# SBUF tiles placed by size, and gate columns with both parts of the activations as one moving operand

## The chip, the core and the metric

One core of a Trainium2 chip runs the whole program. The metric is the device time of one execution in microseconds; of the kernel before there are three runs, 811.55, 812.54 and 812.93 us, median 812.54. A profiled execution took 812.01 us. TensorE (PE) multiplies, with weight loads of its own (PEld), VectorE (DVE) and ScalarE (ACT) do the elementwise work, GpSimd (POOL) helps out, SyncE (SP) issues most transfers.

## What is computed

Two residual layers over 256 tokens of width 2048, in float32, then a norm. Each layer normalises x, projects it, runs an attention over 32 heads of 64, multiplies the result by a SiLU gate that is a further projection z of the same input, and projects back:

```python
def mixer_a(h, w_in, sinks, w_out, cos, sin):
    proj = h @ w_in
    q, k, v, z = jnp.split(proj, [A_WIDTH, A_WIDTH + A_KV_WIDTH, A_WIDTH + 2 * A_KV_WIDTH], axis=-1)
    ...
    o = banded_attention(q, k, v, A_WINDOW, A_QBLOCK, sinks.reshape(A_KV_HEADS, A_GROUP))
    ...
    return (o * jax.nn.silu(z)) @ w_out

def reference(x, ...):
    for i in range(DEPTH):
        h = rmsnorm(x, norm_w[i])
        out = mixer_a(h, ...) if i == 0 else mixer_b(h, ...)
        x = x + out.astype(x.dtype)
    return rmsnorm(x, final_norm_w)
```

Layer B (`mixer_b`) has an attention with three branches (compressed, selected, windowed) and three more pairs of key and value columns, and the same gate z of 2048 columns. Both layers have 2048 columns of q and 2048 of z.

## The kernel before

Products are made in a two-part form of float32: a value v is split into hi, rounded to the matmul's own format (fp32r), and lo = v - hi, and a product is hi x hi + lo x hi + hi x lo, three matmuls that accumulate in one PSUM bank. The activations are kept transposed, in 16 k tiles of 128 rows: `hT` is the layer's normalised input (hT_hi and hT_lo, two tiles of 16 KB a partition), `aT` the gated attention output (aT_hi, aT_lo).

Weights stream. A step (`add_steps`, L559) covers 2 k tiles and 512 columns: one transfer of 512 KB into `raw` (four buffers, issued four steps ahead on SP's queue), an ACT copy into `w_hi` and a DVE subtraction into `w_lo` (three buffers each, two steps ahead, `split`, L541), then two halves of matmuls. A block is 8 steps that fill two banks `acc0` and `acc1`; there are three `acc` banks in all. After the last step a function `post` drains each bank.

Two kinds of blocks exist. A "tok" block (q, key, value and output columns) puts 128 tokens of hT or aT into the array as the stationary operand and streams 512 columns of w. A "feat" block (the gate columns z) is to come out transposed: 128 columns of w are stationary and the 256 tokens of hT_hi or hT_lo are streamed, so a half does for each of its two groups of 128 columns:

```python
for f in range(2):
    fc = (2 * b + f) * P
    PE.matmul(ps[:, f * S:(f + 1) * S], w_[:, fc:fc + P], hT[ai][:, kt, :],
              start=first and f == 0, stop=last, skip_group_check=True)
```

`post_z` (L668) drains such a bank with one DVE product by rbc (the norm's scale, by token), an ACT tanh and a DVE combination.

The order of the program is: layer A's key and value block; for g = 0 to 3 a q block and a z block; four output blocks with aT; layer B's three key and value blocks, with the small projections of its compression between them; again four times q and z; four output blocks. The attention of group g runs in the background, piece by piece behind the half steps (`background`, L469), mostly during the z block of g and the q block that follows. Everything is first recorded and then ordered by a planner (`Plan.order`), which plays the engines with prices and starts on each engine what is ready, in the order of recording; the big matmuls have the lowest rank (`plan.early = LAST`), so the attention goes first where both are ready. On the chip each engine then runs its list in order and waits on semaphores.

SBUF tiles are placed one behind another in the order in which they are first used. So the small ones among them shift the large ones: in the built program hT_hi, hT_lo, w_hi and w_lo start at 256 modulo 512 bytes, raw and x at 192, the key tile kT, qT and sm at 32, aT_hi and aT_lo at 352.

Of the kernel before, what the change touches and what calls it, by code (L numbers as in the profile page):

```python
# [12 lines left out]
F32 = mybir.dt.float32  # L13
# [177 lines left out]
class Plan:  # L191
# [140 lines left out]
def trunk(ctx: ExitStack, tc: tile.TileContext, x, positions, norm_w, final_norm_w,  # L332
# [182 lines left out]
    def hT_pair(i, hT, j):  # L515

        tb = t_bank("xT")
        for k in range(2):
            for t in range(NT):
                PE.transpose(tb[:, 2 * k + t, :], xt[t][:, (2 * j + k) * P:(2 * j + k + 1) * P], ident)  # L520
        src = [tb[:, 2 * k:2 * k + 2, :].rearrange("p a b -> p (a b)") for k in range(2)]
        g = [gT[:, i * KT + 2 * j + k:i * KT + 2 * j + k + 1] for k in range(2)]
        hi = [hT[0][:, 2 * j + k, :] for k in range(2)]
        for k in range(2):
            copy(hi[k], src[k], scale=g[k])
        for k in range(2):
            DVE.scalar_tensor_tensor(hT[1][:, 2 * j + k, :], src[k], g[k], hi[k].bitcast(F32),
                                     op0=OP.mult, op1=OP.subtract)
# [30 lines left out]
    def add_steps(w, width, col0, kind, act, post, before=None):  # L559

        blk = {}

        def mk(i):
            st = Step()
            st.cols = 1024
            st.dma = w_dma(w, i * 2 * P, 2, col0, NB, width)

            def half(b):  # L570
                if before:
                    before(i)
                hT = act()
                if i == 0:
                    blk[b] = acc_bank(f"acc{b}")
                ps = blk[b]
                for kk in range(2):
                    kt = 2 * i + kk
                    wh, wl = (w_[:, kk * NB:(kk + 1) * NB] for w_ in (st.hi, st.lo))
                    for pi, (ai, w_) in enumerate(((0, wh), (1, wh), (0, wl))):  # L580
                        first = kt == 0 and pi == 0
                        last = kt == KT - 1 and pi == 2
                        if kind == "tok":
                            plan.early = LAST
                            PE.matmul(ps, hT[ai][:, kt, b * P:(b + 1) * P], w_, start=first, stop=last)
                            plan.early = 0
                        else:
                            plan.early = LAST
                            for f in range(2):
                                fc = (2 * b + f) * P  # L590
                                PE.matmul(ps[:, f * S:(f + 1) * S], w_[:, fc:fc + P], hT[ai][:, kt, :],
                                          start=first and f == 0, stop=last, skip_group_check=True)
                            plan.early = 0
                if i == KT // 2 - 1:
                    post(b, ps)
            st.halves = [lambda: half(0), lambda: half(1)]
            return st
        for i in range(KT // 2):
            steps.append(mk(i))

# [67 lines left out]
    def post_z(layer, g):  # L668
        def post(b, ps):
            if b == 0:  # L670
                us[layer, g] = sb.tile([P, 4, S], F32, tag="u", name="u", bufs=2)
            u = us[layer, g][:, 2 * b:2 * b + 2, :]
            DVE.tensor_tensor(u, ps.rearrange("p (a b) -> p a b", a=2),
                              rbc[:, None, :].to_broadcast([P, 2, S]), op=OP.mult)
# [3 lines left out]
            if b == 1:  # L678
                flags.add(("z", layer, g))
        return post  # L680

# [173 lines left out]
    add_steps(a_w_in[0], A_IN, 2048, "tok", lambda: hT0,  # L855
              post_kv(0, lambda: kTA, (P, 0), lambda: vA), before=first_block)
    for g in range(NG):
        add_steps(a_w_in[0], A_IN, g * NB, "tok", lambda: hT0, post_q(0, g))
        add_steps(a_w_in[0], A_IN, 2560 + g * NB, "feat", lambda: hT0, post_z(0, g))
# [33 lines left out]
    for j in range(4):  # L893
        add_steps(a_w_out[0], D, j * NB, "tok", lambda: aTA, post_out_a(j),
# [178 lines left out]
    def add_gates():  # L1073
        box = {}

        def mk(i):
# [4 lines left out]
            def half(b):  # L1081
# [3 lines left out]
                for kk in range(4 * b, 4 * b + 4):  # L1085
                    kt = 8 * i + kk
                    wh, wl = (w_[:, kk * 96:(kk + 1) * 96] for w_ in (st.hi, st.lo))
                    for pi, (ai, w_) in enumerate(((0, wh), (1, wh), (0, wl))):
                        PE.matmul(ps[0:96, 0:S], w_, hT[ai][:, kt, :], start=kt == 0 and pi == 0,
# [14 lines left out]
    def b_add(col, kind, post, before=None):  # L1104
        add_steps(b_w_in[0], B_IN, col, kind, hT_b, post, before=before)
# [8 lines left out]
    for g in range(NG):  # L1114
        b_add(g * NB, "tok", post_q(1, g))
        b_add(3680 + g * NB, "feat", post_z(1, g))
# [126 lines left out]
    for j in range(4):  # L1243
        add_steps(b_w_out[0], D, j * NB, "tok", lambda: aTB[0], post_out_b(j),
                  before=out_before(1) if j == 0 else None)
# [91 lines left out]
```

## Time and profile before

| | us |
|---|---|
| runs, median of three | 812.54 |
| profiled execution, whole | 812.01 |
| profiled execution, span from first to last instruction | 810.3 |
| PE busy in the span | 791.3 |
| DVE busy | 546.1 |
| ACT busy | 469.6 |
| POOL busy | 132.1 |
| DMA, mean over the span | 159 GB/s |

Line 217 is the helper that emits every recorded instruction, so groups are told apart by the names of their tiles, out<-in; of a matmul the moving operand is named first and the stationary one second. Matmuls overlap, and a busy time of one, 398 ns, is longer than the distance to the next. That distance is read from starts in a timeline, or from a piece of the chain of waits: its length by its count.

### The profile page before, as it was taken

Reading aid. Unit: us, or ns where it says so; the run is one execution under the profiler, and the core shown is the slowest. Engines: PE = TensorE matmul, PEld = TensorE weight load, DVE = VectorE, ACT = ScalarE, POOL = GpSimd, SP = SyncE. Lnnn points to the kernel's source line nnn. Section 1 sums busy time; section 2 is a strip of 40 time slices with the busy share of each in tenths; the row PEclk is TensorE's granted clock in tenths of the full one; section 3 lists DMA queues with packets and bytes.
Section 4 is the critical chain, followed back from the end, with each engine's and each line's share of the span. In section 5 each row is a group of like instructions: output and inputs, shape, how many; then the busy total and the mean of one; then the engine's idle time right before and its main releaser. Section 6 shows DMA issues by size and latency. Waiting matters only on the chain.

```text
span 810.3 us, 12740 instructions
## 1 busy us (share of the span) xinstructions
PE 791.3 (98%) x4604; PEld 659.2 (81%) x4604; DVE 546.1 (67%) x1116; ACT 469.6 (58%) x931; POOL 132.1 (16%) x169
## 2 busy tenths in 40 slices
PE   7999999999999999999999999999999999999995
PEld 4889879799798788888878898788779769877884
DVE  5646957858668555555756478858948868875562
ACT  6658547456466344454756486567658748654442
POOL 2102211213023000020011022112221022211110
PEclk8999999999999999999999999999999999999998
DMA  8665454554553455565677654444444344454652
GB/s 268 196 177 170 130 170 143 156 157 130 158 180 131 155 182 182 179 190 171 178 228 210 173 163 119 131 131 131 108 143 140 106 130 131 156 156 134 192 168 104
DMA packets 69615, 128.83 MB, mean 159 GB/s; under 512 B 6178, under 2 KB 10497, under 8 KB 69424
## 3 DMA queue, kind: packets, MB, share of 16 engines
q1 hardware_dynamic: 69152, 126.72, 52.3%
q0 software_dynamic: 400, 1.30, 0.6%
q8 instruction: 36, 0.59, 0.3%
q14 instruction: 27, 0.22, 0.1%
HBM read 125.91 MB, written 2.10 MB: 158 GB/s over the span
## 4 chain that ended last, share of the span: by engine, by line
PE 85%; DVE 6%; issue 3%; ACT 2%; POOL 2%; DMA 1%; POOLq 0%; ACTq 0%
PE acc L217 70%; PE pv L217 4%; PE s L217 4%; PE pT L217 3%; DVE sm L217 2%; DVE w_lo L217 2%; PE qT L217 1%; DVE den L217 1%; ACT w_hi L217 1%; POOL sm L217 1%; PE xT L217 1%; DMA pos_i<-in_positions 1%; PE gates L217 1%; PE pcT L217 0%; DVE es L217 0%
## 5 line engine op out<-in xcount | busy, mean ns | idle before, releaser
L217 DVE TENSOR_TENSOR w_lo<-raw,w_hi 128x1024 fp32r<-128x1024 f32 (+1 forms) x231 | 291.1, 1263 | 178.7 <-ACT w_hi L217 174.3
L217 ACT ACTIVATE w_hi<-raw 128x1024 fp32r<-128x1024 f32 (+1 forms) x231 | 241.9, 1050 | 198.0 <-PE acc L217 165.4
L217 PE MATMUL acc<-w_hi,hT_hi 128*128 128x512 f32 x384 | 152.5, 398 | 2.1 <-ACT w_hi L217 2.1
L217 PE MATMUL acc<-w_hi,hT_lo 128*128 128x512 f32 x384 | 152.8, 398 | 0.5 <-DVE hT_lo L217 0.5
L217 PE MATMUL acc<-w_lo,hT_hi 128*128 128x512 f32 x384 | 151.9, 396 | 0.0
L217 PE MATMUL acc<-hT_hi,w_lo 128*128 128x256 f32 x512 | 106.7, 284 | 0.0
L217 PE MATMUL acc<-hT_lo,w_hi 128*128 128x256 f32 x512 | 105.9, 284 | 0.0
L217 PE MATMUL acc<-hT_hi,w_hi 128*128 128x256 f32 x512 | 105.6, 285 | 0.0
L217 PE MATMUL acc<-w_hi,aT_lo 128*128 128x512 f32 x236 | 94.3, 399 | 0.0
L217 PE MATMUL acc<-w_hi,aT_hi 128*128 128x512 f32 x236 | 94.1, 399 | 0.0
L217 PE MATMUL acc<-w_lo,aT_hi 128*128 128x512 f32 x236 | 93.5, 397 | 0.0
L217 PEld LDWEIGHTS acc<-w_hi,hT_hi 128*128 128x128 f32 x384 | 72.4, 189 | 21.4 <-ACT w_hi L217 4.7
L217 PEld LDWEIGHTS acc<-w_hi,hT_lo 128*128 128x128 f32 x384 | 72.5, 189 | 21.1 <-issue 6.5
L217 PEld LDWEIGHTS acc<-w_lo,hT_hi 128*128 128x128 f32 x384 | 72.4, 189 | 16.1 <-issue 2.4
L217 PEld LDWEIGHTS acc<-hT_hi,w_hi 128*128 128x128 f32 x512 | 80.8, 191 | 0.8
L217 PEld LDWEIGHTS acc<-hT_hi,w_lo 128*128 128x128 f32 x512 | 80.6, 191 | 0.0
L217 PEld LDWEIGHTS acc<-hT_lo,w_hi 128*128 128x128 f32 x512 | 80.5, 191 | 0.0
L217 ACT ACTIVATE sm<-sm,nmb 128x128 f32<-128x128 f32 (+1 forms) x128 | 57.0, 446 | 24.4 <-DVE nmb L217 24.3
L217 DVE CUSTOM_DVE_ANT_0 sm<-s,mask 128x128 f32<-128x128 f32 (+1 forms) x128 | 43.5, 349 | 20.4 <-PE s L217 20.1
L217 PEld LDWEIGHTS acc<-w_hi,aT_hi 128*128 128x128 f32 x236 | 44.5, 188 | 12.7 <-issue 1.6
L217 PEld LDWEIGHTS acc<-w_hi,aT_lo 128*128 128x128 f32 x236 | 44.5, 188 | 11.8 <-issue 1.6
L217 PEld LDWEIGHTS acc<-w_lo,aT_hi 128*128 128x128 f32 x236 | 44.5, 188 | 10.3
(191 smaller groups left out, 1009.8 us busy)
## 6 DMA issues: line engine op xcount, KB each, us to landing
raw<-in_b_w_in SPq DMA_DIRECT2D x88, 512.0 KB, 3.6
raw<-in_a_w_in SPq DMA_DIRECT2D x72, 512.0 KB, 3.7
raw<-in_a_w_out SPq DMA_DIRECT2D x32, 512.0 KB, 3.5
raw<-in_b_w_out SPq DMA_DIRECT2D x32, 512.0 KB, 4.0
x<-in_x SPq DMA_DIRECT2D x8, 256.0 KB, 6.8
raw<-in_b_cmp_k_w SPq DMA_DIRECT2D x4, 512.0 KB, 3.8
raw<-in_b_cmp_v_w SPq DMA_DIRECT2D x4, 512.0 KB, 3.8
out<-x SPq DMA_DIRECT2D x4, 512.0 KB, 3.2
```

The source lines that it names most:

```text
L217: return getattr(eng.real, method)(*[real(a) for a in args], **{k: real(a) for k, a in kw.items()})
```

## The change

Three things are edited. `place` allocates every SBUF ring before the program is emitted, those whose size is a multiple of 512 bytes first, largest first, and the others behind them; in the built program all of the first kind then start at 128 modulo 512 (hT, aT, w_hi, w_lo, raw, x, kT, qT, sm and more). hT becomes one tile in which both parts of a k tile lie side by side, and a gate matmul streams both, 512 columns, against w_hi; w_lo then meets the first part alone, 256 columns, in the bank's first half. A bank holds 128 gate columns now, the two halves of it to be added, so a z block of 512 columns becomes two parts of 256 columns, each of 4 steps of 4 k tiles, with two banks each. And `post_z` copies a bank's second half to SBUF (`side`, ACT), adds it to the first (DVE), and after the second bank of a part does the product, tanh and combination for both. Two tiles that reuse old room move: the final gain lies in kT's room, the last weights in that of hT and sm.

```diff
+    def place(self):
+
+        rings = [r for r in self.rings.values() if not r[0].psum]
+        size = {id(r): max(4 * math.prod(b.shape[1:]) for b in r) for r in rings}
+        for r in sorted(rings, key=lambda r: -size[id(r)] if size[id(r)] % 512 == 0 else 0):
+            r[0].real()
+
     def emit(self):
+        self.place()
         for op in self.order():
...
     def new_hT():
-        return (sb.tile([P, KT, S], F32R, tag="hT_hi", name="hT_hi"),
-                sb.tile([P, KT, S], F32R, tag="hT_lo", name="hT_lo"))
+
+        return sb.tile([P, KT, 2, S], F32R, name="hT")
...
         blk = {}
+        nk, ncol = (2, NB) if kind == "tok" else (4, NB // 2)
...
-            st.dma = w_dma(w, i * 2 * P, 2, col0, NB, width)
+            st.dma = w_dma(w, i * nk * P, nk, col0, ncol, width)
...
+                    if kind == "tok":
+                        for pi, (ai, w_) in enumerate(((0, wh), (1, wh), (0, wl))):
+                            PE.matmul(ps, act(ai, kt, b), w_, start=first and pi == 0, stop=last and pi == 2)
+                    else:
+                        fc, hT = slice(b * P, (b + 1) * P), act()
+                        PE.matmul(ps, wh[:, fc], hT[:, kt].rearrange("p a b -> p (a b)"), start=first, stop=False)
+                        PE.matmul(ps[:, 0:S], wl[:, fc], hT[:, kt, 0, :], start=False, stop=last)
+                    plan.early = 0
+                if i == KT // nk - 1:
                     post(b, ps)
...
-    def post_z(layer, g):
+    def post_z(layer, g, part):
         def post(b, ps):
+            if part == b == 0:
+                us[layer, g] = sb.tile([P, 4, S], F32, tag="u", name="u", bufs=2)
+            u = us[layer, g][:, 2 * part + b, :]
+            side = sb.tile([P, S], F32, tag="q32", name="side", bufs=2)
+            copy(side, ps[:, S:2 * S])
+            DVE.tensor_tensor(u, ps[:, 0:S], side, op=OP.add)
             if b == 0:
-                us[layer, g] = sb.tile([P, 4, S], F32, tag="u", name="u", bufs=2)
-            u = us[layer, g][:, 2 * b:2 * b + 2, :]
-            DVE.tensor_tensor(u, ps.rearrange("p (a b) -> p a b", a=2),
-                              rbc[:, None, :].to_broadcast([P, 2, S]), op=OP.mult)
+                return
+            u = us[layer, g][:, 2 * part:2 * part + 2, :]
+            DVE.tensor_tensor(u, u, rbc[:, None, :].to_broadcast([P, 2, S]), op=OP.mult)
...
+    def add_z(w, width, col0, layer, g, act):
+        for part in range(2):
+            add_steps(w, width, col0 + g * NB + part * NB // 2, "feat", act, post_z(layer, g, part))
...
-                gf["t"] = sb.tile([P, KT * S], F32, tag="hT_hi", name="gf")[:, 0:D]
+                gf["t"] = sb.tile([P, 2 * NG * KEYS_B], F32, tag="kT", name="gf")[:, 0:D]
...
-        big = sb.tile([P, KT * S], F32R, tag="hT_lo", name="w_last")
-        yield big[:, 0:1024], big[:, 1024:2048]
-        yield big[:, 2048:3072], big[:, 3072:4096]
-        for tag, bufs in (("sm", 4), ("sm", 4), ("qs", 2)):
-            yield tuple(sb.tile([P, 1024], F32R, tag=tag, name="w_last", bufs=bufs) for _ in range(2))
+        big = sb.tile([P, 8, 1024], F32R, tag="hT", name="w_last")
+        for i in range(4):
+            yield big[:, 2 * i, :], big[:, 2 * i + 1, :]
+        yield tuple(sb.tile([P, 1024], F32R, tag="sm", name="w_last", bufs=4) for _ in range(2))
```

PE's list where layer A's first z block begins, before (a number behind a name tells tiles apart, and x2 two equal rows):

```order
L217 MATMUL acc1_455<-w_hi_574,hT_lo_194 128x512
L217 MATMUL acc1_455<-w_lo_581,hT_hi_172 128x512
L217 MATMUL acc0_631<-hT_hi_172,w_hi_592 128x256 [waits Activation_49]
L217 MATMUL acc0_631<-hT_hi_172,w_hi_592 128x256
L217 MATMUL acc0_631<-hT_lo_194,w_hi_592 128x256 x2
L217 MATMUL acc0_631<-hT_hi_172,w_lo_599 128x256 [waits DVE_49]
L217 MATMUL acc0_631<-hT_hi_172,w_lo_599 128x256
L217 MATMUL acc0_631<-hT_hi_172,w_hi_592 128x256 x2
```

The same place after:

```order
L217 MATMUL acc1_477<-w_hi_595,hT_63 128x512 x2
L217 MATMUL acc1_477<-w_lo_602,hT_63 128x512
L217 MATMUL acc0_652<-hT_63,w_hi_613 128x512 [waits Activation_49]
L217 MATMUL acc0_652<-hT_63,w_lo_620 128x256 [waits DVE_49]
L217 MATMUL acc0_652<-hT_63,w_hi_613 128x512
```

The six matmuls of a k tile and a bank have become two of a k tile and a bank of half as many columns: 12 a k tile and block before, 8 after.

DVE's list where that z block ends, before (`u` is the gate, `pt` and `w_lo` are other work, `u<-u,pv` is the product with the attention):

```order
L217 TENSOR_TENSOR w_lo_1025<-raw_815,w_hi_1009 128x1024 [waits DMAHW3_49,PE_49,Activation_49]
L217 TENSOR_TENSOR u_1039<-acc0_631,rbc_369 128x512 [waits PE_49]
L217 TENSOR_TENSOR pt_1048<-pT_1023,part_137 128x512
L217 TENSOR_TENSOR u_1039<-acc1_653,rbc_369 128x512 [waits PE_49]
L217 TENSOR_TENSOR w_lo_1066<-raw_872,w_hi_1053 128x1024 [waits DMAHW4_49,Activation_49]
L217 SCALAR_TENSOR_TENSOR u_1039<-th_1063,u_1039 128x512 [waits Activation_49]
```

The same place after, where the second part of the block ends:

```order
L217 TENSOR_TENSOR u_75<-acc0_813,side_995 128x256 [waits Activation_49]
L217 RECIPROCAL den_941<-den_941 128x4 [waits DVE_49]
L217 TENSOR_TENSOR pt_1011<-pT_991,part_84 128x512
L217 TENSOR_TENSOR pt_1021<-pT_991,part_84 128x512
L217 TENSOR_TENSOR w_lo_1028<-raw_860,w_hi_1017 128x1024 [waits DMAHW4_49,PE_49,Activation_49]
L217 TENSOR_TENSOR u_75<-acc1_905,side_1025 128x256 [waits Activation_49]
L217 TENSOR_TENSOR pt_1045<-pT_1035,part_84 128x512
L217 TENSOR_TENSOR u_75<-u_75,rbc_85 128x512 [waits DVE_49]
```

A drain on DVE waits for ACT's copy now instead of PE alone, and the product with rbc follows after both banks.

PE's list in the middle of that z block, after, where the second bank of the second part (`acc1_905`) is first written; it is the bank that `acc0_652` of the first part had:

```order
L217 MATMUL acc0_813<-hT_63,w_hi_820 128x512
L217 MATMUL s_886<-kTA_64,qT_749 128x256 [waits Activation_49]
L217 MATMUL s_886<-kTA_64,qT_749 128x256 x3
L217 MATMUL s_892<-kTA_64,qT_749 128x256 [waits DVE_49]
L217 MATMUL s_892<-kTA_64,qT_749 128x256 x3
L217 MATMUL pT_898<-cst_91,sm_801 128x128 [waits PE_49,Pool_49]
L217 MATMUL pT_898<-cst_91,sm_801 128x128 x3
L217 MATMUL acc1_905<-hT_63,w_hi_727 128x512 [waits DVE_49]
L217 MATMUL acc1_905<-hT_63,w_lo_747 128x256
```

Before, no bank changes in the middle of a z block. Now the planner has put three steps of the part's first bank ahead of the second bank's first matmul.

## Rows read from the trace of the kernel before

**Rows 1.** The page: busy time by engine; shares of the chain that ended last.
```profile
PE 791.3 (98%) x4604; PEld 659.2 (81%) x4604; DVE 546.1 (67%) x1116; ACT 469.6 (58%) x931; POOL 132.1 (16%) x169
...
PE 85%; DVE 6%; issue 3%; ACT 2%; POOL 2%; DMA 1%; POOLq 0%; ACTq 0%
```

**Rows 2.** The chain in order of time: start us, length us, what, count.
```profile
69.50 3.43 PE acc L217 x28
...
73.76 3.47 PE acc L217 x29
...
90.33 1.92 POOL sm L217
...
285.79 22.27 PE acc L217 x95
...
362.26 9.76 PE acc L217 x43
...
731.94 58.54 PE acc L217 x250
```

**Rows 3.** PE's timeline, 69 to 71 and 598 to 599: start us, us, instruction.
```profile
69.66 0.41 PE L217 MATMUL acc<-hT_hi,w_hi 128*128 128x256 f32 x2
...
70.85 0.40 PE L217 MATMUL acc<-hT_hi,w_lo 128*128 128x256 f32 x2
...
597.91 0.40 PE L217 MATMUL acc<-w_hi,hT_hi 128*128 128x512 f32 x1
...
599.08 0.39 PE L217 MATMUL acc<-w_lo,hT_hi 128*128 128x512 f32 x1
```

**Rows 4.** Groups by shape, the last of 61.4 to 91.4: count, busy us, mean ns.
```profile
L217 PE MATMUL acc<-w_hi,hT_hi 128*128 128x512 f32 x384 | 152.5, 398 | 2.1 <-ACT w_hi L217 2.1
...
L217 PE MATMUL acc<-hT_hi,w_hi 128*128 128x256 f32 x512 | 105.6, 285 | 0.0
...
L217 PE MATMUL acc<-w_hi,aT_hi 128*128 128x512 f32 x236 | 94.1, 399 | 0.0
...
L217 PE MATMUL acc<-w_last,aT_hi 128*128 128x512 f32 x40 | 12.9, 396 | 0.0
...
L217 PE MATMUL acc<-w_last,aT_lo 128*128 128x512 f32 x20 | 7.9, 395 | 0.0
...
L217 DVE TENSOR_TENSOR low<-s,mask 128x256 f32<-128x256 f32 x16 | 6.7, 421 | 5.4 <-PE s L217 5.1
...
L217 DVE TENSOR_TENSOR w_lo<-raw,w_hi 128x1024 fp32r<-128x1024 f32 x8 | 9.9, 1240 | 5.6 <-ACT w_hi L217 5.6
```

**Rows 5.** Tiles rbc and u: ns min/median/max; who waited for u.
```profile
L217 ACT ACTIVATE rbc<-rbc x2: 384/384/385, 28.9 to 362.3; 128x256 f32<-128x256 f32 x2
...
L217 DVE TENSOR_TENSOR u<-acc,rbc x16: 680/682/692, 91.3 to 708.8; 128x512 f32<-128x512 f32 x16
...
  PEld s L217: 0.8, 1
```

**Rows 6.** Stretches: busy us by engine, granted clock, DMA share, GB/s.
```profile
29.00:41.00 12.00, 12.00 (x54) 9.74 (x52) 0.48 (x1) 0.93 (x2) 1.00 0.67 200
...
61.40:91.40 30.00, 30.00 (x251) 29.02 (x249) 22.68 (x60) 21.73 (x53) 11.00 (x14) 1.00 0.50 142
...
257.00:353.00 96.00, 95.50 (x422) 75.25 (x421) 55.57 (x63) 44.42 (x60) 0.89 (x1) 1.00 0.54 175
...
533.00:567.00 34.00, 34.00 (x277) 31.81 (x277) 25.98 (x88) 26.34 (x70) 7.78 (x11) 1.00 0.49 140
```

**Rows 7.** Transfers: queue, count, KB each, median us from issue to landing.
```profile
raw<-in_a_w_in SPq DMA_DIRECT2D x72, 512.0 KB, 3.7
...
raw<-in_b_cmp_k_w SPq DMA_DIRECT2D x4, 512.0 KB, 3.8
```

**Rows 8.** Waits: who for whom, us in total, times, longest.
```profile
PE pT L217 <- POOL sm L217: 2.0, 4, 0.5
...
ACT w_last L217 <- DMA raw<-in_b_w_out: 2.0, 2, 1.8
```

More of the change, by code (lines that the diff above doesn't have):

```diff
@@ L522, in hT_pair @@
         g = [gT[:, i * KT + 2 * j + k:i * KT + 2 * j + k + 1] for k in range(2)]
-        hi = [hT[0][:, 2 * j + k, :] for k in range(2)]
+        hi = [hT[:, 2 * j + k, 0, :] for k in range(2)]
         for k in range(2):
@@ L526, in hT_pair @@
         for k in range(2):
-            DVE.scalar_tensor_tensor(hT[1][:, 2 * j + k, :], src[k], g[k], hi[k].bitcast(F32),
+            DVE.scalar_tensor_tensor(hT[:, 2 * j + k, 1, :], src[k], g[k], hi[k].bitcast(F32),
                                      op0=OP.mult, op1=OP.subtract)
@@ L572, in half @@
                     before(i)
-                hT = act()
                 if i == 0:
@@ L576, in half @@
                 ps = blk[b]
[L577 to L594, printed above, removed]
+                for kk in range(nk):
+                    kt = nk * i + kk
+                    wh, wl = (w_[:, kk * ncol:(kk + 1) * ncol] for w_ in (st.hi, st.lo))
+                    first, last = kt == 0, kt == KT - 1
+                    plan.early = LAST
+                    if kind == "tok":
[7 more added lines that the diff above has]
+                if i == KT // nk - 1:
                     post(b, ps)
@@ L597, in mk, with of_hT, of_aT @@
             return st
-        for i in range(KT // 2):
+        for i in range(KT // nk):
             steps.append(mk(i))
+    def of_hT(hT):
+        return lambda ai, kt, b: hT()[:, kt, ai, b * P:(b + 1) * P]
+    def of_aT(aT):
+        return lambda ai, kt, b: aT()[ai][:, kt, b * P:(b + 1) * P]
     def rope(v, t, nh):
@@ L677, in post @@
             DVE.scalar_tensor_tensor(u, th, 1.0, u, op0=OP.add, op1=OP.mult)
-            if b == 1:
+            if part == 1:
                 flags.add(("z", layer, g))
         return post
+    def add_z(w, width, col0, layer, g, act):
+        for part in range(2):
+            add_steps(w, width, col0 + g * NB + part * NB // 2, "feat", act, post_z(layer, g, part))
     def new_aT():
@@ L853, in trunk @@
     first_done = set()
-    add_steps(a_w_in[0], A_IN, 2048, "tok", lambda: hT0,
+    add_steps(a_w_in[0], A_IN, 2048, "tok", of_hT(lambda: hT0),
               post_kv(0, lambda: kTA, (P, 0), lambda: vA), before=first_block)
     for g in range(NG):
-        add_steps(a_w_in[0], A_IN, g * NB, "tok", lambda: hT0, post_q(0, g))
-        add_steps(a_w_in[0], A_IN, 2560 + g * NB, "feat", lambda: hT0, post_z(0, g))
+        add_steps(a_w_in[0], A_IN, g * NB, "tok", of_hT(lambda: hT0), post_q(0, g))
+        add_z(a_w_in[0], A_IN, 2560, 0, g, lambda: hT0)
     nA = len(steps)
@@ L893, in trunk @@
     for j in range(4):
-        add_steps(a_w_out[0], D, j * NB, "tok", lambda: aTA, post_out_a(j),
+        add_steps(a_w_out[0], D, j * NB, "tok", of_aT(lambda: aTA), post_out_a(j),
                   before=out_before(0) if j == 0 else None)
@@ L1088, in half @@
                     for pi, (ai, w_) in enumerate(((0, wh), (1, wh), (0, wl))):
-                        PE.matmul(ps[0:96, 0:S], w_, hT[ai][:, kt, :], start=kt == 0 and pi == 0,
+                        PE.matmul(ps[0:96, 0:S], w_, hT[:, kt, ai, :], start=kt == 0 and pi == 0,
                                   stop=kt == KT - 1 and pi == 2)
@@ L1104, in b_add @@
     def b_add(col, kind, post, before=None):
-        add_steps(b_w_in[0], B_IN, col, kind, hT_b, post, before=before)
+        add_steps(b_w_in[0], B_IN, col, kind, of_hT(hT_b), post, before=before)
     aTB = []
@@ L1115, in trunk @@
         b_add(g * NB, "tok", post_q(1, g))
-        b_add(3680 + g * NB, "feat", post_z(1, g))
+        add_z(b_w_in[0], B_IN, 3680, 1, g, hT_b)
     nB = len(steps)
@@ L1243, in trunk @@
     for j in range(4):
-        add_steps(b_w_out[0], D, j * NB, "tok", lambda: aTB[0], post_out_b(j),
+        add_steps(b_w_out[0], D, j * NB, "tok", of_aT(lambda: aTB[0]), post_out_b(j),
                   before=out_before(1) if j == 0 else None)
     def last_rooms():
-        big = sb.tile([P, KT * S], F32R, tag="hT_lo", name="w_last")
-        yield big[:, 0:1024], big[:, 1024:2048]
-        yield big[:, 2048:3072], big[:, 3072:4096]
-        for tag, bufs in (("sm", 4), ("sm", 4), ("qs", 2)):
-            yield tuple(sb.tile([P, 1024], F32R, tag=tag, name="w_last", bufs=bufs) for _ in range(2))
+        big = sb.tile([P, 8, 1024], F32R, tag="hT", name="w_last")
+        for i in range(4):
+            yield big[:, 2 * i, :], big[:, 2 * i + 1, :]
+        yield tuple(sb.tile([P, 1024], F32R, tag="sm", name="w_last", bufs=4) for _ in range(2))
     rooms = last_rooms()
```

## Prediction

> **What bounds the kernel now.** I read the page's first part and its chain first. PE is busy for 791.3 of 810.3 us, DVE for 546.1 and ACT for 469.6, and 85% of the chain that ended last is PE [rows 1]. A busy PE need not be a PE at its peak, so the next view to read is the chain in order of time, where it stays on PE for long pieces: a piece's length over its count is the time from one matmul's start to the next, the pitch, which is what a matmul really costs. Three pitches stand there [rows 2]. A 512-column matmul whose stationary operand is hT takes 9.76 / 43 = 227 ns. One whose stationary operand is aT takes 22.27 / 95 = 234.4 ns and 58.54 / 250 = 234.2 ns. The 256-column matmuls of the gate columns take 122.5 ns in one piece (3.43 / 28) and 119.7 in another (3.47 / 29); inside a piece ten of them go from 69.66 to 70.85, 119 ns each [rows 3]. I use 120. So 256 columns cost more than half of 512: 2 x 120 = 240 against 227. The granted clock is 1.00 in the stretches of all three kinds [rows 6], and none of this is the clock.
>
> With these pitches the big matmuls alone take 1536 x 0.120 + 1152 x 0.227 + 768 x 0.234 = 184 + 262 + 180 = 626 us, counts from [rows 4] (3 x 512 for the gates, 3 x 384 for the other input columns, 3 x 236 + 40 + 20 for the two output projections). The rest of PE is attention. Whatever shortens the pitch of these 3456 matmuls shortens the kernel, as long as ACT and DVE keep delivering.
>
> **The change part by part. First, the merged operand.** Per k tile and 128 gate columns there were three 256-column matmuls: w_hi with hT_hi, w_hi with hT_lo, w_lo with hT_hi. Now there are one of 512 columns (w_hi with both) and one of 256. The streamed columns are the same, 768; 512 matmuls and as many weight loads are gone. Each merged pair costs 227 instead of 240 ns: 13 ns, and 512 x 13 = **6.7 us**. No row shows a 512-column matmul with w stationary and hT moving. The bounds are 2 x 120 - 234 = 6 ns (3.1 us) and 2 x 122.5 - 227 = 18 ns (9.2 us); I take 13, since both operands then stand in the same relation as in the 227 ns row.
>
> The rows price a matmul at its columns over 2.4 GHz (213 and 107 ns) plus 13 to 14 ns, whatever its width. The Trainium skill's page "TensorE: Matmul & The Clock Gate" (section "Back-to-back issue gap") gives N / 2.4 + 2.5 ns for a warm matmul; an estimate by that page is 512 x 2.5 ns = 1.3 us for this part instead of 6.7. The trace does not agree with it here, and the row decides.
>
> **Second, the placement.** Before, hT, w_hi and w_lo lie at 256 modulo 512 bytes, aT at 352. After, all tiles of a multiple of 512 bytes lie at 128, so aT agrees with w as hT does today. The pitch of hT (227) and of aT (234.3) differ by 7.3 ns, and I can see nothing else that differs: same shapes, same instruction, same clock, in stretches where PE waits for nothing. If agreement is the cause, 768 x 7.3 = **5.6 us**. It is not the whole cause: with the very same hT tiles five matmuls right behind a pv group go from 597.91 to 599.08, 234 ns each [rows 3]; so the relation in time between two streams matters too, and agreement only makes the good state likely. The two output projections run in pieces of 95 and 250 matmuls, with long room to settle, as the 43 at 227 do, so I take the full 5.6. The bounds are 0 and 5.6 as a gain; as a loss, if it is the residue itself and not the agreement that counts, see the third rival.
>
> Operands that keep 4 passes or are transposes (pT, xT, pv) get new residues too. They make up a small part and I put them at 0. Of DVE and ACT I expect nothing either.
>
> **Third, what the halves cost elsewhere.** The two parts of the activations no longer add up in PSUM. Per 128 gate columns ACT copies the second half to SBUF and DVE adds it to the first: 32 copies and 32 additions in all, for 16 parts (8 blocks, two parts each). Nearest rows: the ACT copy of the same shape from PSUM, rbc, 384 ns [rows 5]; the DVE addition of the same shape with one PSUM input, low, 421 ns [rows 4]. That is 32 x 0.384 = 12.3 us on ACT and 32 x 0.421 = 13.5 us on DVE. The product with rbc remains, 16 x 0.68 [rows 5], now from SBUF. In a gate stretch of layer A DVE goes from 22.68 of 30.00 us (76%) to 24.4 of 29.1 (84%), in layer B from 25.98 of 34.00 to 27.7 of 33.1 (84%), ACT there from 26.34 to 27.9 [rows 6]. Both still have 5 us to spare per stretch, so most of it is hidden.
>
> What is not hidden is a matter of the three banks. A bank now has to be drained by two engines, and twice per block instead of once. New work goes on in the third bank for one half step, 4 x (227 + 120) = 1.39 us. If a split (w_lo, 1.24 us) [rows 4] stands ahead, the drain takes 1.24 + 0.384 + 0.421 = 2.05 us, 0.65 late. Queued behind the waiting DVE addition are then w_lo of a later step and the softmax, and behind PE's wait all of PE. Before, of 16 drains only one made anybody on PE wait, 0.8 us [rows 5]. In the new order PE does three steps of the part's first half and a run of s and pT before it asks for the late bank, far more than 1.39 us. Bounds: 0, and 32 x (0.384 + 0.421) = 25.8 us if every drain stood bare. I take **2 us**, three of the sixteen parts late by 0.65.
>
> One wait may vanish: four times a pT waits 0.5 us for POOL's sm, 2.0 in sum [rows 8], in layer A at the end of a gate block; the matmuls between its scores and it are spread otherwise now. I leave these 2 us out, as the other side of the same uncertainty.
>
> **At nothing:** the gate weights come in rows of 1 KB instead of 2 KB. The loads of kc's and vc's first weights have such rows, 3.8 us to landing against 3.7 [rows 7]; four loads are ahead, some 11 us of steps, and the DMA share is 0.49 to 0.50 in gate stretches [rows 6]. If that cover were gone, the splits would wait for raw, which they do only at the very end now, twice, 2.0 us in sum [rows 8]. The last weights lie in hT instead of hT_lo, sm and qs, and the final gain in kT: these tiles are dead by then, and POOL's queue holds only the one load behind that wait.
>
> **The sum.** The profiled execution took 812.0 us (its span 810.3 and 1.7 around it), 0.5 below the median of the runs. 812.0 - 6.7 - 5.6 + 2.0 = 801.7, and against the median 802.2.
>
> **The rivals.** *Placement does nothing.* The pitch of aT would stay at 234: 812.5 - 6.7 + 2.0 = 807.8. For it speaks the slow state of hT in [rows 3], which needs no different residue. Against it: 95 and 250 in a row without one fast stretch, while hT has 43 in a row at 227 [rows 2]. The Trainium skill, in the same page's "Step-by-step: what each phase is for", says that the load of the next weights does not steal SBUF read bandwidth from the running matmul; by that rule this rival is the outcome. The traces bear it out badly: equal instructions differ by 7 ns.
>
> *The drains come onto the path.* ACT and DVE at 84% in order, with two-engine drains, make PE wait at most part ends: 16 x 0.65 = 10.4 us instead of 2, which gives 810.6. For it: DVE's and ACT's share; in layer A the chain already leaves PE for POOL's sm near the block's end [rows 2]. Against it: PE itself loses only half a us there [rows 8].
>
> *The residue, not the agreement, is what counts,* and 128 is a bad one. Then all 512-column matmuls of the kernel run at 234.3. Merging gains 512 x (240 - 234.3) = 2.9 us, the other 1152 of hT lose 7.3 ns each, 8.4 us, aT gains nothing: 812.5 - 2.9 + 8.4 + 2.0 = 820.0, slower. With p as the common pitch the gain is (512 x 240 + 1152 x 227 + 768 x 234.3) - 2432 x p, so it becomes a loss without the drains at p = 232.1. Against it speaks that no row ties a residue by itself to a pitch; for it, that 227 is only seen at residue 256.
>
> **How the numbers follow.** The forecast, 802.2 with 798 to 806 as its own range, 0.66. Placement does nothing, 0.14 (806 to 809). Drains on the path, 0.13 (806 to 812, a fifth of it above 811). The residue, 0.06. A rest of 0.01 below 797. About 0.2%, 1.6 us, is what a measurement of this kernel can tell from no change. Faster by more than that, below 810.9: 0.66 + 0.14 + 0.10 + 0.01 = 0.91; within it 0.03; slower 0.06. The range from 798 to 809 holds most of the forecast, the first rival and half of the second, some 0.8.
>
> **What would show it.** In the chain of the changed kernel, the output projections' long pieces at 227 to 229 ns per matmul (234 if placement does nothing), kv columns at 227 (234 if the residue counts), and the gate matmuls in turn 227 and 120 apart in the timeline. In the waits, PE's acc for DVE's u: up to 2 us in sum, 10 if the drains are on the path. DVE some 13 and ACT some 12 us busier. Wrong would be the forecast if the merged matmul took 240 or more, or if the pitch of aT came out anywhere but at that of hT.

## The result, and the profile after

The changed kernel takes 800.65 us (median of 4 runs, 800.08 to 801.18), the kernel before in the same session 812.44; the ratio is 0.9857 with an interval of 0.9842 to 0.9872. That is 11.8 us less, against 10.3 forecast (802.2, range 798 to 809). The profiled execution took 801.2 us, 1.7 of it outside its span.

The page of the changed kernel, busy time by engine, and the shares of its chain of waits:

```profile
PE 783.0 (98%) x4092; PEld 631.8 (79%) x4092; DVE 553.8 (69%) x1148; ACT 479.1 (60%) x963; POOL 125.5 (16%) x169
...
PE 92%; DVE 3%; issue 2%; ACT 1%; DMA 1%; POOL 1%; SPq 0%; ACTq 0%; POOLq 0%; DVEq 0%
```

Against [rows 1] PE is still busy 98% of the time, with 512 instructions less; the kernel is shorter because a busy PE got more done. The chain is now on PE for 92% instead of 85%.

The chain in order of time (start us, length us, what, count) shows the pitch of long pieces, to be read against [rows 2]: first the end of layer A's first gate block, where [rows 2] had POOL's sm for 1.92 us, then a long piece of each of the two output projections:

```profile
85.96 4.07 PE acc L217 x22
90.02 0.44 PE pT L217 x4
90.46 3.48 PE acc L217 x17
93.94 0.03 issue
93.97 0.66 PE pT L217 x4
94.63 5.92 PE acc L217 x26
...
280.34 21.57 PE acc L217 x95
...
725.46 54.52 PE acc L217 x239
```

A matmul with aT as stationary operand takes 21.57 / 95 = 227.1 ns and 54.52 / 239 = 228.1 ns, where it took 234. At the end of the gate block the chain stays on PE.

PE's timeline in a gate block (start us, us, instruction) shows the merged pairs one behind the other:

```profile
63.60 0.40 PE L217 MATMUL acc<-hT,w_hi 128*128 128x512 f32 x1
63.83 0.28 PE L217 MATMUL acc<-hT,w_lo 128*128 128x256 f32 x1
63.95 0.40 PE L217 MATMUL acc<-hT,w_hi 128*128 128x512 f32 x1
64.19 0.28 PE L217 MATMUL acc<-hT,w_lo 128*128 128x256 f32 x1
64.31 0.40 PE L217 MATMUL acc<-hT,w_hi 128*128 128x512 f32 x1
...
66.07 0.40 PE L217 MATMUL acc<-hT,w_hi 128*128 128x512 f32 x1
```

From 63.60 to 66.07 lie seven pairs, (66.07 - 63.60) / 7 = 353 ns each. The forecast had 347. From one start to the next it is 230 to 240 ns for the 512 columns and 120 for the 256.

The drains, by the view of the tile `side` (ns min, median, max):

```profile
L217 ACT ACTIVATE side<-acc x32: 359/365/380, 78.1 to 691.8; 128x256 f32<-128x256 f32 x32
L217 DVE TENSOR_TENSOR u<-acc,side x32: 393/412/425, 79.1 to 693.7; 128x256 f32<-128x256 f32 x32
```

A copy takes 365 ns and an addition 412, somewhat less than the neighbours from which they were estimated (384 and 421): 11.7 us in all on ACT, 13.2 on DVE. From the list of waits (who for whom: us in total, times, longest), and the landing time of the gate weights:

```profile
DVE u L217 <- ACT side L217: 5.7, 4, 1.5
...
PE acc L217 <- ACT aT_hi L217: 0.8, 1, 0.8
...
PE acc L217 <- DVE aT_lo L217: 0.2, 1, 0.2
PE pT L217 <- DVE sm L217: 0.2, 1, 0.2
...
raw<-in_a_w_in SPq DMA_DIRECT2D x72, 512.0 KB, 3.6
```

DVE waits 5.7 us for ACT's copies, but in the whole list there is no line of PE's acc for DVE's u. PE's pT no longer waits for POOL's sm, which was 2.0 us in [rows 8]. New is 1.0 us at the start of layer B's output projection, for aT_hi and aT_lo. The 72 loads of that line mix rows of 1 and 2 KB; layer A's 32 gate loads by themselves, taken from the trace, land after 3.5 us in the median, against 3.7 before.

### The profile page after: what moved, and what is told of

The parts are those of the page before. It is cut to its first block, busy times and chain, and to the rows that moved or that the text cites. A ratio compares the mean times of both kernels' runs of the same rounds, so it can differ in the third digit from the quotient of the medians.

```text
span 799.5 us, 11784 instructions
## 1 busy us (share of the span) xinstructions
PE 783.0 (98%) x4092; PEld 631.8 (79%) x4092; DVE 553.8 (69%) x1148; ACT 479.1 (60%) x963; POOL 125.5 (16%) x169
## 4 chain that ended last, share of the span: by engine, by line
PE 92%; DVE 3%; issue 2%; ACT 1%; DMA 1%; POOL 1%; SPq 0%; ACTq 0%; POOLq 0%; DVEq 0%
PE acc L217 75%; PE pv L217 5%; PE s L217 4%; PE pT L217 4%; PE qT L217 1%; DVE w_lo L217 1%; PE xT L217 1%; DMA raw<-in_a_w_in 1%; DVE sm L217 1%; ACT w_hi L217 1%; PE gates L217 1%; PE pcT L217 0%; PE kT L217 0%; PE mlp L217 0%; POOL rope L217 0%
## 5 line engine op out<-in xcount | busy, mean ns | idle before, releaser
L217 PE MATMUL acc<-w_hi,hT 128*128 128x512 f32 x768 | 247.6, 398 | 2.3 <-ACT w_hi L217 1.7
L217 PE MATMUL acc<-hT,w_hi 128*128 128x512 f32 x512 | 186.4, 399 | 0.0
L217 PEld LDWEIGHTS acc<-w_hi,hT 128*128 128x128 f32 x768 | 142.9, 189 | 37.9 <-issue 4.9
L217 PE MATMUL acc<-w_lo,hT 128*128 128x512 f32 x384 | 152.1, 396 | 0.0
L217 PE MATMUL acc<-hT,w_lo 128*128 128x256 f32 x512 | 143.7, 283 | 0.0
L217 PEld LDWEIGHTS acc<-hT,w_hi 128*128 128x128 f32 x512 | 96.2, 188 | 21.3 <-issue 3.2
L217 PEld LDWEIGHTS acc<-hT,w_lo 128*128 128x128 f32 x512 | 96.6, 189 | 0.7
L217 PEld LDWEIGHTS acc<-w_lo,hT 128*128 128x128 f32 x384 | 72.7, 189 | 18.5 <-issue 4.9
L217 POOL TENSOR_TENSOR sm<-sm,denb 128x512 f32<-128x512 f32 (+1 forms) x16 | 29.3, 1832 | 151.2 <-DVE mx L217 60.8
L217 PE MATMUL s<-kTB,qT 128*128 128x272 f32 x192 | 39.2, 295 | 0.0
L217 PE MATMUL pT<-cst,sm 128*128 128x128 f32 x256 | 37.9, 275 | 0.5 <-DVE sm L217 0.2
```

The costliest lines, as they stand in the source:

```text
L217: return getattr(eng.real, method)(*[real(a) for a in args], **{k: real(a) for k, a in kw.items()})
```

## The experiments

The theory was that the gain is the sum of two separate things: the placement (7 ns on each of 768 matmuls, because stationary and moving operand agree in address) and the merging (fewer, wider matmuls). Rivals: only one of the two does it; the absolute residue counts, not the agreement; the drains cost much more or nothing. In all numbers below the kernel before is the one run beside the experiment. Where an experiment changes addresses alone, the order of instructions on PE is exactly that of the kernel that it starts from: of the kernel before for e1, of the changed kernel for e2, e4, e5, e6 and e8.

**Placement alone, and merging alone.** `e1_place_only` is the kernel before with the new allocation and nothing else.

```diff
+    def place(self):
+        rings = [r for r in self.rings.values() if not r[0].psum]
+        size = {id(r): max(4 * math.prod(b.shape[1:]) for b in r) for r in rings}
+        for r in sorted(rings, key=lambda r: -size[id(r)] if size[id(r)] % 512 == 0 else 0):
+            r[0].real()
+
     def emit(self):
+        self.place()
```

> The kernel before with the placement rule alone; gate columns as before. Theory (the pitch of aT falls because aT then agrees with w): output projections at 227 to 228 ns per matmul instead of 234, 768 x 6.9 ns = 5.3 us, so 807.1 us; gate and hT pitches unchanged at 120 and 227. Rival (the 5 us in the changed kernel's output projections came with the merged order, not with the placement): 234 ns stay, 812.4 us.

Measured: 807.08 us (806.23 to 807.31), 0.9933 of before (0.9916 to 0.9949), 5.2 us less.

`e2_merge_only` is the changed kernel in which the two aT rings come last, behind three small ones of 96 bytes together, so that aT stands 96 bytes off w modulo 256, as it did before.

```diff
+        late = ('aT_hi', 'aT_lo')
         for r in sorted(rings, key=lambda r: -size[id(r)] if size[id(r)] % 512 == 0 else 0):
+            if size[id(r)] % 512 == 0 and r[0].tag not in late:
+                r[0].real()
+        by = {r[0].tag: r for r in rings}
+        for tag in ('warm', 'pos_i', 'nhalf') + late:
+            by[tag][0].real()
+        for r in rings:
             r[0].real()
```

> The changed kernel with aT_hi and aT_lo alone moved by 96 bytes against w, as they stood before; all other large tiles agree as in the changed kernel. Theory: output projections back at 234 ns, 5.3 us lost, 806.0 us; the rest as in the changed kernel, so merging is worth 6.4 us by itself, somewhat more than its matmuls alone (4 to 5 us by the pitches). Rival (what the placement gains is something else than aT against w): 800.7 us. Rival two (parts are not additive, the drains take back what one brings): off 806.0 by 2 us or more.

Measured: 805.37 us (805.04 to 806.18), 0.9916 (0.9902 to 0.9931), 6.9 us less. The chain of e1 and then of e2, in order of time, at the same output projection:

```profile
285.24 21.59 PE acc L217 x95
```
```profile
279.93 22.25 PE acc L217 x95
```

227.3 ns with placement, 234.2 without. Each part alone brings what it brings in the whole: 5.2 + 6.9 = 12.1, together 11.8. "Placement does nothing" is out, and e2, which moves aT alone, shows that it is aT against w that counts and not the other tiles that `place` moves.

**Residue or agreement, and what agreement means.** `e8_all192` moves all large tiles to residue 192 by putting one ring of 64 bytes ahead of them; the next three move aT and hT against w, by small rings put ahead of them: aT +32 and hT +64 bytes (`e4_off32_64`), +128 and +256 (`e5_off128_256`), -32 and -64 (`e6_offm32_m64`).

```diff
 e8:
+        first = {r[0].tag: r for r in rings}["ang"]
+        first[0].real()
         for r in sorted(rings, key=lambda r: -size[id(r)] if size[id(r)] % 512 == 0 else 0):
             r[0].real()
 e4 (e5: 'sinks' and 'nsink' as the small rings; e6: more of them):
...
+        late = ("aT_hi", "aT_lo", "hT")
+        for r in sorted(rings, key=lambda r: -size[id(r)]):
+            if size[id(r)] % 512 == 0 and r[0].tag not in late:
+                r[0].real()
+        for tag in ('warm',) + late[:2] + ('pos_i',) + late[2:]:
+            by[tag][0].real()
...
```

> The changed kernel with all large tiles moved by 64 bytes together, to 192 modulo 512, so that they agree as before among themselves. Theory (the relation of stationary and moving operand counts, not the residue): 227.3 and 228.4 ns in output projections and key, value and q columns, 800.7 us. Rival (the residue itself counts, and multiples of 128 are the good ones): 233 in both, 812 us.

> The changed kernel with aT moved by 32 bytes and hT by 64 bytes against w. Theory (any disagreement modulo 512 puts the pitch at 234): output projections at 234 (plus 5.3 us), key, value and q columns at 234 (1152 x 6 = 7 us more), gate matmuls slower too; 812 to 816 us. Rival (only the place in a smaller unit counts, 64 bytes say): hT stays at 227 and aT goes to 234, 806 us; with a unit of 32 bytes both stay at 227, 801 us.

> The changed kernel with aT moved by 128 bytes and hT by 256 bytes against w. With 32 and 64 bytes both pitches were 233.2 ns. Theory (512 bytes is the unit, any disagreement in it costs the same): output projections 234, key, value and q columns 233, some 808 to 811 us. Rival (the unit is 128 or 256 bytes): at 256 hT has 228 ns again, and with a unit of 128 aT has 227 too; 806 or 801 us.

> The changed kernel with aT moved 32 bytes down and hT 64 bytes down against w (480 and 448 upwards). Theory (agreement is a single good point): 233 to 234 ns in both, 807 to 810 us. Rival (the weight load must not trail the stream, the direction counts): one sign costs and the other doesn't, so both at 227 or faster, 801 us or less.

Measured, one execution each: e8 800.58 us, e4 809.27, e5 804.13, e6 807.13; that of the changed kernel was 801.18. The chains in order of time; e8, e4, e5 and e6. The piece at 29 us is matmuls with hT as stationary operand, that at 280 with aT:

```profile
28.91 12.26 PE acc L217 x54
...
279.74 21.57 PE acc L217 x95
```
```profile
29.30 12.60 PE acc L217 x54
...
282.94 22.16 PE acc L217 x95
```
```profile
28.97 12.26 PE acc L217 x54
...
280.26 22.07 PE acc L217 x95
```
```profile
29.43 12.37 PE acc L217 x54
...
281.71 22.16 PE acc L217 x95
```

12.26 / 54 = 227.0, 12.60 / 54 = 233.3, 12.37 / 54 = 229.1 ns. Over whole kernels, the mean distance from the start of one of the big matmuls (those into acc) to the next one's, where no other matmul stands between and the distance is under 300 ns, worked out from the starts in the traces, with the offset of the stationary operand from w in bytes:

| kernel | aT offset | aT 512 cols, ns | hT offset | hT 512 cols, ns | gate 512, ns | gate 256, ns |
|---|---|---|---|---|---|---|
| before | 96 | 234.1 | 0 | 228.4 | - | 121.3 |
| after | 0 | 227.3 | 0 | 228.4 | 234.6 | 120.2 |
| placement alone (e1) | 0 | 227.3 | 0 | 228.1 | - | 121.4 |
| merging alone (e2) | 96 | 234.2 | 0 | 228.4 | 234.6 | 120.4 |
| all at 192 (e8) | 0 | 227.4 | 0 | 228.4 | 234.5 | 120.2 |
| e4 | 32 | 233.3 | 64 | 233.2 | 231.7 | 122.1 |
| e5 | 128 | 232.5 | 256 | 228.3 | 234.6 | 120.2 |
| e6 | -32 | 233.3 | -64 | 229.7 | 233.5 | 121.7 |
| gates grouped (e3) | 0 | 227.2 | 0 | 228.3 | 231.6 | 121.4 |
| without w_lo (e9) | 0 | 227.4 | 0 | 228.9 | 230.1 | - |

Three residues (256 for hT before, 128 after, 192 in e8) give the same pitch, so the residue by itself is not what counts. An offset of 256 is as good as none and one of 128 is not, so of the offsets tried the unit is 256 bytes and not 512 or 128. Everything else tried costs 1 to 7 ns per matmul. The times follow: e4 is 8.1 us slower than the changed kernel. Its pitches would make it 768 x 6.0 + 1152 x 4.8 = 10.1 us, less the 0.5 that its gate pairs gain (512 x (2.9 - 1.9)); with every distance counted, breaks and waits too, the output projections take 4.1 us more and the matmuls with hT 4.4.

**The drains.** `e7_no_side` leaves out ACT's copy and DVE's addition of the second half; DVE copies the first half instead, so the product of w_hi with the activations' lo part is missing from the gates.

```diff
-            side = sb.tile([P, S], F32, tag="q32", name="side", bufs=2)
-            copy(side, ps[:, S:2 * S])
-            DVE.tensor_tensor(u, ps[:, 0:S], side, op=OP.add)
+            DVE.tensor_copy(u, ps[:, 0:S])
```

> The changed kernel without the drain's two new instructions: ACT's copy of the bank's second half and DVE's addition are left out and DVE copies the first half alone, so the gate lacks the product with the activations' lo part. Theory (the drains are hidden, PE never waits for them): 800.7 us, within 0.5. Rival (they cost the 2 us that the prediction put down, or more): 798.7 us or less.

Measured: 799.02 us (798.18 to 799.41), 0.9831 (0.9814 to 0.9847): 1.6 us less than the changed kernel and near the rival's number, 1.8 between the two spans (799.5 and 797.7). The intervals of the two ratios overlap, though all four runs of e7 lie below all of the changed kernel. But the planner also came to another order without the two instructions: PE's list differs from the changed kernel's at about a hundred places. So 1.6 us is the drains and the new order together, and how much is the drains' own is not shown; 10 is excluded. As idle time of PE little of it shows: summed over PE's groups it is 10.4 us before, 7.9 in the changed kernel and 7.4 in e7.

**The pitch of the merged matmul.** It came out at 234.6 and not at 227, with both operands in agreement. A gate matmul of 512 columns always stands between two of 256, so two experiments change what stands around it. `e3_grouped` orders the four k tiles of a gate half as four of 512 and then four of 256.

```diff
-                for kk in range(nk):
+                for kk in range(nk if kind == "tok" else 2 * nk):
+                    ai, kk = divmod(kk, nk)
...
-                        PE.matmul(ps, wh[:, fc], hT[:, kt].rearrange("p a b -> p (a b)"), start=first, stop=False)
-                        PE.matmul(ps[:, 0:S], wl[:, fc], hT[:, kt, 0, :], start=False, stop=last)
+                        if ai == 0:
+                            PE.matmul(ps, wh[:, fc], hT[:, kt].rearrange("p a b -> p (a b)"), start=first, stop=False)
+                        else:
+                            PE.matmul(ps[:, 0:S], wl[:, fc], hT[:, kt, 0, :], start=False, stop=last)
```

> The changed kernel; in a gate half the four 512-column matmuls come first, then the four of 256, instead of in turn. In the changed kernel a gate matmul of 512 columns takes 233 to 235 ns and one of 256 117 to 120, 355 the pair on average, where 347 was forecast. Theory one (the change of width from one to the next keeps the streams out of step): grouped they run at 227 and 120, 347 the pair, 512 x 8 = 4 us less, 796.6 us. Theory two (w as the stationary operand at 512 columns is slower by itself): 234 and 120, 800.7 us as without grouping.

Measured: 798.46 us (798.09 to 799.52), 0.9832 (0.9817 to 0.9847), between the two numbers. PE's timeline of e3:

```profile
63.71 1.09 PE L217 MATMUL acc<-hT,w_hi 128*128 128x512 f32 x4
64.64 0.64 PE L217 MATMUL acc<-hT,w_lo 128*128 128x256 f32 x4
65.11 0.80 PE L217 MATMUL qT<-identr,qs 128*128 128x128 f32 x8
```

(64.64 - 63.71) / 4 = 233 ns, (65.11 - 64.64) / 4 = 118: in this group of four hardly anything is gained yet; over all, the mean went from 234.6 to 231.6.

`e9_no_wlo` leaves the 256-column matmuls out altogether, so the product with w_lo is missing from the gates, and the 512-column ones follow each other without a break.

```diff
-                        PE.matmul(ps, wh[:, fc], hT[:, kt].rearrange("p a b -> p (a b)"), start=first, stop=False)
-                        PE.matmul(ps[:, 0:S], wl[:, fc], hT[:, kt, 0, :], start=False, stop=last)
+                        PE.matmul(ps, wh[:, fc], hT[:, kt].rearrange("p a b -> p (a b)"), start=first, stop=last)
```

> The changed kernel without the 256-column gate matmuls (w_lo with the activations' hi part is left out), so that the 512-column ones with w stationary stand in an unbroken stream. In turn with 256 columns they took 234.6 ns, grouped in fours 231.6. Theory one (the change of width keeps the streams out of step): 227 to 228 ns here. Theory two (w stationary and both parts streaming is slower by itself): 234. The time falls by some 512 x 0.12 = 61 us, to 740 us, if the splits keep up; ACT and DVE have then 84% more to do per gate time, so waits for w_lo's split or the drains may take back some of it.

Measured, one execution: 770.38 us. PE's timeline, a run of 18 behind each other, and the shares of its chain:

```profile
60.96 4.25 PE L217 MATMUL acc<-hT,w_hi 128*128 128x512 f32 x18
```
```profile
PE 66%; DVE 14%; ACT 6%; POOL 6%; issue 5%; DMA 1%; SPq 0%; POOLq 0%; ACTq 0%; DVEq 0%
```

Less the 0.40 that a single one lasts, 17 distances take 3.85 us: 226 ns. So the same matmul with the same tiles does run at 227 in a long run of its own width; in turn with 256 columns it takes 233 to 235. Over all of e9 the mean is 230.1, because most runs are short (the last section has the course of a run). The forecast of the total, 740, was far off: 512 x 0.120 = 61 us of PE went and the kernel lost only 31. The windows of the changed kernel say a part of why (stretch, then busy us of PE, PEld, DVE, ACT, POOL, clock, DMA share, GB/s), for a gate stretch of layer A and one of B:

```profile
62.20:91.40 29.20, 29.20 (x185) 25.27 (x184) 23.59 (x62) 23.19 (x57) 9.42 (x13) 1.00 0.45 128
524.90:557.70 32.80, 32.80 (x208) 27.75 (x207) 26.52 (x91) 26.21 (x71) 4.61 (x7) 1.00 0.46 130
```

There are eight such stretches, so 61 / 8 = 7.7 us of PE went from each. DVE alone is busy for 23.6 of 29.2 and 26.5 of 32.8 us, so a stretch could shrink by 5.6 and 6.3 us at most, even if DVE never waited. In e9 the chain does lie on DVE, ACT and POOL for 26%, and PE's idle time, summed as above, is 29.3 us instead of 7.9. Two of its waits, and the windows of two of its stretches, one behind the other:

```profile
PE pT L217 <- POOL sm L217: 5.0, 8, 0.9
PE acc L217 <- DVE u L217: 3.4, 4, 0.9
```
```profile
688.00:694.00 6.00, 4.33 (x19) 1.88 (x19) 2.38 (x4) 2.77 (x4) 0.00 (x0) 1.00 0.00 0
694.00:697.40 3.40, 3.40 (x10) 2.62 (x9) 0.55 (x1) 1.42 (x2) 0.00 (x0) 0.50 0.43 132
```

With PE faster, the wait for a late bank that the changed kernel's list lacks does appear, 3.4 us. And waiting costs a second time. Before 694 us PE had waited 1.44 us for aT_hi and 0.23 for aT_lo; then the granted clock fell from 1.00 to 0.50, from 2.4 to 1.2 GHz, and the eight 512-column matmuls that start from 694.24 to 697.22 stand 427 ns apart instead of 227, which costs 1.4 us. Two other stretches of e9, from 76.2 and from 588.2 us, show 0.50 too, behind waits for sm, nm and nmb of 0.2 to 0.9 us each. The three together cost some 4 us, an estimate from the one. In the traces of all other kernels the granted clock is 1.00 from 18 us on to the last 9 us.

**Grouping, once more beside the changed kernel.** `e10_grouped_again` is the kernel of e3, and `e11_after_again` the changed kernel, on the same chip.

> The grouped kernel once more, beside the changed kernel on one chip, since 798.5 and 800.7 us came from different calls and lie within each other's intervals. Theory (grouping gains): 798.5 us, 0.25 to 0.3% below the changed kernel. Rival (the difference was the chip's): the same as the changed kernel within 0.1%.

> The changed kernel itself, as the partner of the grouped one: 800.7 us.

Measured: 799.32 us (798.74 to 799.45), 0.9843 (0.9829 to 0.9858), and 800.75 (800.54 to 801.15), 0.9863 (0.9847 to 0.988). All four runs of the grouped kernel lie below all four of the changed one, by 1.4 us between the medians, 0.18%. The ratios' intervals overlap, so it is a small gain that the runs agree on, not a large one. The two profiled executions lie 2.0 us apart. Of that the gate matmuls make 0.4 us (183.4 to 183.0, each from its start to the next start on PE, breaks included), the output projections 0.9 (178.2 to 177.3) and the matmuls with hT 0.8 (274.7 to 273.9). So most of the gain lies outside the gates, where PE's order came out a little otherwise. The one wait that can be named for it is that for aT_hi, here in the groups by shape (count, busy us, mean ns, idle us before) of the changed kernel and of e3:

```profile
L217 PE MATMUL acc<-w_hi,aT_hi 128*128 128x512 f32 x236 | 92.9, 394 | 0.8 <-ACT aT_hi L217 0.8
```
```profile
L217 PE MATMUL acc<-w_hi,aT_hi 128*128 128x512 f32 x236 | 92.7, 393 | 0.0
```

Of the kernels that compute everything it is the fastest that was run: 0.984 of the kernel before.

## Why the prediction came out right, step by step

**The reading of the bound was right.** PE was the bound with its pitch, not its busy share, and every part of the change that shortened a pitch shortened the kernel.

**Placement: right, in size and cause.** Forecast 768 x 7.3 = 5.6 us; e1 alone gave 5.2, and the pitches 768 x 6.8 = 5.2. The chain's 95 and 250 in a row at 234 were the argument against the rival "placement does nothing", and it held. The Trainium skill's page "TensorE: Matmul & The Clock Gate" (section "Step-by-step: what each phase is for") says that loading the next weights takes no SBUF read bandwidth from the running matmul, and the rival concluded from it that placement does nothing. That conclusion does not fit this case: the kernel before and e1 have the same instructions in the same order on PE, and the output projections differ by 7 ns per matmul through addresses alone. Whether it is the weight loads that take the time, no run here shows. At nothing the prediction also put the other operands that got new residues, and that held: s, pv and pT take 38.2, 38.2 and 25.4 us in the kernel before and in e1 alike, from start to start. The rival "the residue counts" fell by the changed kernel itself (228.4 at residue 128 for hT) and by e8. What was wrong in the words, at no cost in time, is "modulo 512": the offset of 256 in e5 costs nothing.

**Merging: the mechanism was right, the term was mis-sized, and by two errors.** The step that failed is "each merged pair costs 227 instead of 240 ns: 13 ns": since both operands stand in the relation of the 227 ns row, I took its pitch. The merged matmul takes 234.6, the end of the range at which the term is smallest (234), because a neighbour of another width keeps it there (226 to 227 in a long run of e9). Against it the old matmuls cost 121.3 in the mean, not 120. By the pitches the term is 512 x (3 x 121.3 - 234.6 - 120.2) = 512 x 9.1 = 4.7 us; by all distances from a gate matmul's start to the next start, breaks included, the gates went from 187.1 us in e1 to 183.5, which is 3.6. So the term was 2 to 3 us too large.

**What made up for it: the wait that was left out.** From e1 to the changed kernel the span lost 6.1 us, and the gate matmuls make only 3.6 of it. In the same sum of distances, the matmuls with hT as stationary operand went from 277.1 to 274.9 (a wait of PE counts to the matmul ahead of it), s from 38.2 to 37.1, pv from 38.2 to 37.6; pT rose from 25.4 to 26.2 and the output projections from 177.5 to 178.2. Most of that first fall comes from the end of layer A's gate blocks, where the chain of e1 still leaves PE, once for each of the four (two are shown). Three of the four waits have a matmul with hT ahead of them, the last one has an output projection:

```profile
89.32 0.93 DVE den L217
90.59 1.92 POOL sm L217
...
144.49 0.93 DVE den L217
145.76 1.92 POOL sm L217
```

In the changed kernel no such piece is left. It is the wait of pT for POOL's sm, 2.0 us in [rows 8], which the prediction named as one that "may vanish" and left out. Behind the rise of the output projections is the new wait for aT_hi and aT_lo, 1.0 us, which nothing in the prediction names. What shortened s and pv was not traced. Two mistakes of 2 to 3 us with opposite signs leave the sum where it was, 801.7 forecast for a profiled execution and 801.2 measured. That the sum is this close is luck; that both parts are worth several us is not.

**The drains: the number is near, the mechanism did not occur.** Forecast 2 us, as PE's acc waiting for a late bank. PE waits for no bank in the changed kernel; e7 gives 1.6 to 1.8 us, but with another order on PE, and only 0.5 us of it shows as idle time of PE. Where the rest sits the runs do not show, so the term of 2 us is neither confirmed nor refuted. "Drains on the path" with 10 us is out. The gate stretches came out at 81% of DVE and 79 to 80% of ACT instead of 84. The additions and copies took 13.2 and 11.7 us, against 13.5 and 12.3 forecast, and the engines' other work stayed what it was in sum: added up one by one, DVE's instructions lasted 609.5 us before and 621.6 after, ACT's 527.1 and 539.1, 12 us more each. The busy times rose by only 7.7 and 9.5, since they count stretches in which the records of two instructions overlap once.

**At nothing: right.** Layer A's loads in smaller rows land after 3.5 us and layer B's after 3.7, both 3.7 before, and the split at the end waits for raw about as long as before (2.3 us now, against 2.0).

```profile
ACT w_last L217 <- DMA raw<-in_b_w_out: 2.3, 2, 1.8
```

## What to carry to other kernels

Where an engine is busy all the time, divide a long piece of the chain by its count and compare like with like: two groups of the same shape with different pitches are a lead, and here it was worth 5 us for a change of addresses alone. Lay out the tiles that meet as stationary and moving operand so that their addresses agree modulo 256 bytes, and put matmuls of one width next to each other, in runs of a dozen or more if the order allows it: groups of four brought the gate matmuls here only 0.4 us. When a pitch is forecast from a row, take it from a row whose neighbours have the same shapes too, and do not leave out a wait that the change removes because another term is uncertain by as much.

## What the runs showed that I had not expected

A matmul's pitch depends on its neighbour's width and on its place in a run of its own kind. The merged gate matmul takes 226 to 227 ns late in a long run, 233 to 235 in turn with 256 columns and 231.6 in the mean in groups of four. The traces show why four do not get there. The mean distance by place in an unbroken run of 512-column matmuls of one kind (same kind of stationary operand, under 300 ns, from the starts in the traces):

| kind, kernel | offset | 1st to 4th, ns | 5th to 8th | 9th to 12th | from the 13th |
|---|---|---|---|---|---|
| hT, after | 0 | 232.1 | 229.4 | 227.6 | 226.7 |
| aT, after | 0 | 231.8 | 230.7 | 228.1 | 226.7 |
| gate, without w_lo (e9) | 0 | 232.8 | 228.7 | 227.0 | 226.7 |
| gate, grouped (e3) | 0 | 232.0 | - | - | - |
| hT, e6 | -64 | 232.0 | 229.2 | 229.4 | 229.0 |
| aT, before | 96 | 233.2 | 234.4 | 233.8 | 234.2 |
| hT, e4 | 64 | 232.8 | 233.4 | 233.3 | 233.3 |

Every run begins at 232 to 233. With agreeing addresses it settles to 226.7 over about a dozen matmuls, at -64 to 229, and at 64 and 96 it stays where it began or rises a little. A group of four is over before it has settled, and the five matmuls at 234 behind a pv group, which the prediction found in [rows 3], stand at the beginning of a run as well. So agreement does not make a matmul fast, it lets a long run become fast, as the prediction had suspected; what in the chip settles, the runs do not show.

The relation of addresses works modulo 256 bytes, and not evenly: hT at -64 takes 229.7 ns, at +64 233.2; and at +64, where hT as stationary operand is slow, the gate matmul in which hT is the moving one is faster, 231.7 against 234.6, though its partner of 256 columns is slower, 122.1 against 120.2. The runs show these sizes and not the mechanism behind them.
